# Sliding windows by DMA alone: twelve staged batches in place of eleven, and copies in fewer, larger DMAs

## The chip, the cores and the metric

The kernel runs on one core of a Trainium2 chip. The metric is the device time of one execution in microseconds (us), lower is better. A core has 16 DMA engines that move the data; SP (SyncE), ACT (ScalarE) and POOL (GpSimd) issue DMAs into queues of their own, called q1, q10 and q0 in the profile. [...]

## What is computed

The input `x` has 32 batches of 4096 rows of 256 float32 values. Windows of 64 rows are taken every 32 rows, 127 to a batch, and copied out one after the other:

```python
n_windows = (length - window_size) // stride + 1
result = np.zeros((batch, n_windows, window_size, dim), dtype=np.float32)
for i in range(n_windows):
    start = i * stride
    result[:, i] = x[:, start:start + window_size].copy()
```

Neighbouring windows share half of their rows. With blocks of 32 rows (32 KB), batch `b` has 128 blocks, and window `w` is block `w` (its half 0) followed by block `w + 1` (its half 1). The output has 127 x 2 blocks per batch, 266.3 MB in all. There is no arithmetic.

## The kernel before

There are two ways for a batch to get to the output. A *direct* batch is copied from HBM to HBM: each output block is one read and one write. A *staged* batch is loaded once into a tile of SBUF, `xb0` to `xb5`, with block `p` in partition `p`, and the tile is stored twice, once as the half 0 of all windows and once as the half 1.

A tile holds 128 blocks, but there are 127 windows. Each store thus writes one block too many, into the last window of the batch before or the first of the batch behind. The direct copies leave out some windows next to a staged batch, the *edges*, and write them once the stores that spill into them have landed.

Eleven batches are staged, 1, 4, ... 31 (L121), the other 21 are direct. Three queues work side by side:

- ACT (`ring_s`) runs `Staging.run` (L96 to L103): six loads, then the twelve stores of these tiles, then five loads, then ten stores. A load into a tile that was used before waits for its stores (`stored`, L83), a store for its load (`loaded`, L88). A load or a store is one DMA of 4 MB whose packets are 16 KB (`IN`, `OUT`, L9).
- SP (`ring_d`) copies 112 windows of each direct batch, 16 windows at a time (L144 to L162). Either one DMA moves both halves (`windows`, L29) or two DMAs move one half each. The counter `share` chooses: the second form is used often while ACT loads and seldom while it stores. Packets are 32 KB.
- POOL (`ring_r`) waits for the semaphore `near`, which counts a DMA just before the end of SP's list (L164), and then copies the edges in order of batches, 15 windows a DMA. Before each edge it waits for the stores that spill into it (`wait_stored`, L170).

At the end POOL copies most of the last direct batch's edge, part of it in 4 KB pieces (`columns`, L40, L179). SP waits for the stores of the last tile (L180), copies the last two windows, which such a store spilled into, as `columns` too (L181), and waits for all semaphores (L182, L183).

Of the kernel before, what the change touches and what calls it, by code (L numbers as in the profile page):

```python
# [6 lines left out]


DIRECT, IN, OUT = 32768, 16384, 16384  # L9


class Copier:


    def __init__(self, x, out, B, L, D, W, S, n_win):
        assert W == 2 * S and L % S == 0
        self.x, self.out = x, out
        self.B = B
        self.blk = S * D
        self.nb = L // S  # L20
        self.nw = n_win
# [7 lines left out]
    def windows(self, q, b, w0, n, half=None, piece=DIRECT):  # L29
# [7 lines left out]
            max_dma_last_dim=piece,  # L37
        )

    def columns(self, q, b, w0, n):  # L40

        part = self.blk // 8
        row = [1, part]
        return q.dma_start(  # L44
            out=self.oap((b * self.nw + w0) * 2, [[part, 16], [2 * self.blk, n], row]),
            in_=self.xap(b * self.nb + w0, [[part, 16], [self.blk, n], row]),
        )

    def load(self, q, t, b, shift):

        return q.dma_start(
            out=t[:, :],
            in_=self.xap(b * self.nb - shift, [[self.blk, self.nb], [1, self.blk]]),
            max_dma_last_dim=IN,
        )

    def store(self, q, t, b, half, shift):


        w = b * self.nw - half - shift  # L60
        return q.dma_start(
            out=self.oap(2 * w + half, [[2 * self.blk, self.nb], [1, self.blk]]),
            in_=t[:, :],
            max_dma_last_dim=OUT,
        )


class Staging:


    def __init__(self, c, tc, pool, dtype, batches, bufs, shifts):
        self.c, self.batches, self.shifts = c, batches, shifts
        self.tiles = [pool.tile([128, c.blk], dtype, name=f"xb{i}") for i in range(bufs)]
        self.loaded = [tc.alloc_semaphore(f"loaded{i}") for i in range(bufs)]
        self.stored = [tc.alloc_semaphore(f"stored{i}") for i in range(bufs)]

    def shift(self, g):
        return self.shifts.get(self.batches[g], 0)

    def load(self, q, g):  # L80
        n, i = divmod(g, len(self.tiles))
        if n:
            q.wait_ge(self.stored[i], 32 * n)  # L83
        self.c.load(q, self.tiles[i], self.batches[g], self.shift(g)).then_inc(self.loaded[i], 16)

    def store(self, q, g):
        n, i = divmod(g, len(self.tiles))
        q.wait_ge(self.loaded[i], 16 * (n + 1))  # L88
        for half in (0, 1):
            self.c.store(q, self.tiles[i], self.batches[g], half, self.shift(g)).then_inc(self.stored[i], 16)  # L90

    def wait_stored(self, q, g):
        n, i = divmod(g, len(self.tiles))
        q.wait_ge(self.stored[i], 32 * (n + 1))  # L94

    def run(self, q):  # L96
        bufs = len(self.tiles)
        for first in range(0, len(self.batches), bufs):
            group = range(first, min(first + bufs, len(self.batches)))
            for g in group:  # L100
                self.load(q, g)
            for g in group:
                self.store(q, g)  # L103


@with_exitstack
def kernel(
    ctx: ExitStack,
    tc: tile.TileContext,
    x: bass.AP,  # L110
    window_size: bass.AP,
    stride: bass.AP,
    out: bass.AP,
):
    nc = tc.nc
    W, S = int(window_size), int(stride)
    B, L, D = x.shape
    n_win = (L - W) // S + 1
    assert out.shape == (B, n_win, W, D)
    c = Copier(x, out, B, L, D, W, S, n_win)  # L120
    staged = [*range(1, B, 3)]  # L121
    direct = [b for b in range(B) if b not in staged]
    pool = ctx.enter_context(tc.tile_pool(name="xb", bufs=1))

    st = Staging(c, tc, pool, x.dtype, staged, 6, {0: -1, B - 1: 1})
    ring_d, ring_s, ring_r = nc.sync, nc.scalar, nc.gpsimd
    done = tc.alloc_semaphore("done")
    near = tc.alloc_semaphore("near")  # L130
    rest = tc.alloc_semaphore("rest")
    total = {done: 0, near: 0, rest: 0}

    def count(dma, sem):
        dma.then_inc(sem, 16)
        total[sem] += 16

    per, loads, stores = 6, 6 * 17, 34
    todo = 7 * len(direct)
    turns = share = 0  # L140
    with tc.tile_critical():  # L141
        st.run(ring_s)

        for b in direct:  # L144
            w = 0 if b - 1 not in staged else 8 if b + 1 in staged and b + 1 < B - 1 else 15
            for j in range(7):
                todo -= 1
                sem = near if todo == 2 else done
                share += 90 if turns % (loads + per * stores) < loads else 12
                if share >= 120:  # L150
                    share -= 120
                    turns += 4
                    count(c.windows(ring_d, b, w, 16, 0), done)
                    count(c.windows(ring_d, b, w, 16, 1), sem)
                else:
                    turns += 3
                    count(c.windows(ring_d, b, w, 16), sem)
                w += 16
                if todo == 7:
                    count(c.windows(ring_d, B - 1, c.nw - 1, 1, 1, 2048), done)  # L160
                    if 0 in staged:
                        count(c.windows(ring_d, 0, 0, 1, 0, 2048), done)  # L162

        ring_r.wait_ge(near, 16)  # L164
        pieces = (32768,)
        last = B - 2
        for i, b in enumerate(direct[:-1]):
            for g, n in enumerate(staged):
                if abs(n - b) == 1:
                    st.wait_stored(ring_r, g)  # L170
            parts = [(0, 15)] if b - 1 in staged else [(112, 15)]
            if b - 1 in staged and b + 1 in staged:
                parts = [(0, 8), (120, 7)]
            for w, n in parts:
                count(c.windows(ring_r, b, w, n, None, pieces[i % len(pieces)]), rest)


        count(c.windows(ring_r, last, 112, 4), rest)
        count(c.columns(ring_r, last, 116, 9), rest)  # L179
        st.wait_stored(ring_d, len(staged) - 1)  # L180
        count(c.columns(ring_d, last, 125, 2), done)  # L181
        for sem in (done, near, rest):  # L182
            ring_d.wait_ge(sem, total[sem])  # L183


# [33 lines left out]
```

## Time and profile before

| what | value |
|---|---|
| median of nine runs | 745.01 us (743.46 to 747.39) |
| the profiled execution | 745.01 us |
| its span, first to last instruction | 743.2 us |
| loads from ACT | 11 DMAs of 4096 KB, median 123.3 us from issue to landing |
| stores from ACT | 22 DMAs of 4096 KB, 141.7 us |
| copies from SP, both halves | 96 DMAs of 1024 KB, 100.3 us |
| copies from SP, one half | 102 DMAs of 512 KB, 90.0 us |
| edges from POOL | 20 DMAs of 960 KB, 37.7 us, and two smaller ones |
| wait of POOL for `near` | 646.4 us |

The profile lists every packet that a DMA engine moved, with its queue, size and duration, but not its engine. Its tables of slices and stretches add these packets up: "DMA share" is the sum of their durations over 16 engines' time, "GB/s" the bytes. Neighbouring packets of one engine overlap by a few nanoseconds, so a share can read 1.01. The packets under 512 B are semaphore writes, 16 for each DMA. The time from issue to landing is long because a DMA waits in its ring behind those issued before it.

### The profile page before, as it was taken

How to read it: one execution, taken by the hardware profiler on the slowest of the kernel's cores; microseconds unless marked ns; L12 is line 12 of the kernel's file. 1: busy time of each engine (PE TensorE's matmuls, PEld its weight loads, DVE VectorE, ACT ScalarE, POOL GpSimd, SP SyncE). 2: the span in 40 equal slices, each digit the busy share in tenths (PEclk: the TensorE clock that was granted, in tenths of full speed). 3: DMA queues.
4: the chain of work that ended last, by engine and by line, in shares of the span. 5: the costliest groups of instructions: out<-in, count | busy, mean ns of one | idle time of the engine just before them, and what ended most of it. 6: DMA issues, size and time to landing. Idle time of an engine off the chain costs nothing.

```text
span 743.2 us, 309 instructions
## 1 busy us (share of the span) xinstructions
POOL 12.8 (2%) x26
## 2 busy tenths in 40 slices
POOL 0000000000000000000000000000000000130100
DMA  8999999999999999999999999999999999999995
GB/s 369 433 429 423 430 433 429 431 421 434 424 423 425 430 419 426 430 421 432 424 429 416 409 428 433 436 428 435 430 431 427 424 433 429 426 429 433 424 431 240
DMA packets 18098, 313.26 MB, mean 421 GB/s; under 512 B 4144, under 2 KB 4144, under 8 KB 4336
## 3 DMA queue, kind: packets, MB, share of 16 engines
q1 hardware_dynamic: 7952, 154.32, 48.8%
q10 hardware_dynamic: 8976, 138.41, 44.0%
q0 software_dynamic: 1168, 20.51, 6.5%
q14 instruction: 2, 0.02, 0.0%
HBM read 220.95 MB, written 267.09 MB: 657 GB/s over the span
## 4 chain that ended last, share of the span: by engine, by line
another core or an unknown queue 92%; POOL 2%; issue 0%; POOLq 0%; SPq 0%
POOL out_dram L34 2%; POOL out_dram L44 0%; POOLq L214 0%; POOLq L94 0%; SPq L141 0%
## 5 line engine op out<-in xcount | busy, mean ns | idle before, releaser
L34 POOL DMA_DIRECT2D out_dram<-in_x_dram x21 | 12.0, 575 | 686.2 <-DMA out_dram<-in_x_dram 646.4
L44 POOL DMA_DIRECT2D out_dram<-in_x_dram x1 | 0.6, 581 | 0.0
L200 POOL MEMSET const-float32-0.0<- 128x1 f32 x1 | 0.1, 98 | 0.2 <-issue 0.2
L200 POOL MEMSET const-bfloat16-1.0<- 128x1 bf16 x1 | 0.1, 101 | 0.0
L200 POOL MEMSET const-uint8-127<- 128x1 uint8 x1 | 0.1, 99 | 0.0
L200 POOL MEMSET const-float32-1.0<- 128x1 f32 x1 | 0.1, 98 | 0.0
## 6 DMA issues: line engine op xcount, KB each, us to landing
out_dram<-in_x_dram SPq DMA_DIRECT2D x96, 1024.0 KB, 100.3
out_dram<-xb ACTq DMA_DIRECT2D x22, 4096.0 KB, 141.7
out_dram<-in_x_dram SPq DMA_DIRECT2D x102, 512.0 KB, 90.0
xb<-in_x_dram ACTq DMA_DIRECT2D x11, 4096.0 KB, 123.3
out_dram<-in_x_dram POOLq DMA_DIRECT2D x20, 960.0 KB, 37.7
out_dram<-in_x_dram POOLq DMA_DIRECT2D x1, 576.0 KB, 40.4
out_dram<-in_x_dram POOLq DMA_DIRECT2D x1, 256.0 KB, 36.9
out_dram<-in_x_dram SPq DMA_DIRECT2D x1, 128.0 KB, 2.4
```

The lines of the kernel that those rows point to most:

```text
L34: return q.dma_start(out=self.oap((b * self.nw + w0) * 2 + h, [[2 * blk, n], row]), in_=self.xap(b * self.nb + w0 + h, [[blk, n], row]), m ...
L44: return q.dma_start(out=self.oap((b * self.nw + w0) * 2, [[part, 16], [2 * self.blk, n], row]), in_=self.xap(b * self.nb + w0, [[part, 16 ...
L200: nc = _bacc.Bacc("TRN2", target_bir_lowering=False, num_devices=1)
```

## The change

- Twelve batches are staged, 0, 3, 6, 9, 11, ... 31, and twenty direct. Batch 0 is loaded one block further on and batch 31 one block further back, so that nothing spills over the ends of the tensors; one block of each is copied alone (`singles`).
- Loads and stores have packets of 32 KB. A load is two DMAs, one for the even and one for the odd partitions (`split(2)`); a store is two of each half in the same way. The stores of the last three tiles are eight DMAs per half, each of 16 partitions, every eighth one (`split(8)`).
- The stores of the last tile are ordered anew: half 1 first, then an eighth of half 0, all counted by `stored`; the other seven eighths are counted by a new semaphore, `ended`. SP's last two windows wait for `stored` alone.
- SP's copies are made by `many`: one DMA moves one half of 112 windows, 7 packets on each of 16 engines. The counter `share` is gone, and so are the DMAs with both halves. The last of these DMAs is cut in two, and `near` counts the second-last.
- The edge of the last direct batch is 3 whole windows and 10 in `columns`, in place of 4 and 9; the others are as before for the new set of batches.
- `quarters` is defined but not called.

```diff
-DIRECT, IN, OUT = 32768, 16384, 16384
+DIRECT, IN, OUT, REST = 32768, 32768, 32768, 32768
...
+    def many(self, q, b, w0, n, half):
+        return q.dma_start(
+            out=self.oap((b * self.nw + w0) * 2 + half, [[2 * self.blk, 16], [32 * self.blk, n], [1, self.blk]]),
+            in_=self.xap(b * self.nb + w0 + half, [[self.blk, 16], [16 * self.blk, n], [1, self.blk]]),
+        )
...
+    def load(self, q, t, b, c, rows):
+        p, step, n, unit = rows
+        return q.dma_start(
+            out=t[p : p + (n - 1) * step + 1 : step, :],
+            in_=self.xap(b * self.nb + c + p // unit, [[step // unit * self.blk, n], [1, self.blk]]),
             max_dma_last_dim=IN,
         )
...
+    def store(self, q, t, b, c, rows, half):
+        p, step, n, unit = rows
+        w = b * self.nw + c + p // unit - half
+        return q.dma_start(
+            out=self.oap(2 * w + half, [[2 * step // unit * self.blk, n], [1, self.blk]]),
+            in_=t[p : p + (n - 1) * step + 1 : step, :],
             max_dma_last_dim=OUT,
         )
...
     def load(self, q, g):
...
+        i = g % len(self.tiles)
+        if self.count[self.stored[i]]:
+            q.wait_ge(self.stored[i], self.count[self.stored[i]])
+        for rows in self.split(2):
+            self.issue(self.c.load(q, self.tiles[i], *self.items[g], rows), self.loaded[i])
+        self.after_load[g] = self.count[self.loaded[i]]
+
+    def split(self, parts):
+        return [(k, parts, 128 // parts, 1) for k in range(parts)]
 
     def store(self, q, g):
...
+        q.wait_ge(self.loaded[i], self.after_load[g])
+        split = self.split(8 if g >= len(self.items) - 3 else 2)
+        parts, end = [(rows, half) for half in (0, 1) for rows in split], []
+        if g == len(self.items) - 1:
+            parts = [(rows, 1) for rows in split] + [(split[0], 0)]
+            end = split[1:]
+        for rows, half in parts:
+            self.issue(self.c.store(q, self.tiles[i], *self.items[g], rows, half), self.stored[i])
+        for rows in end:
+            self.issue(self.c.store(q, self.tiles[i], *self.items[g], rows, 0), self.ended)
...
-    staged = [*range(1, B, 3)]
+    staged = [0, 3, 6, 9, 11, 14, 17, 20, 22, 25, 28, 31]
+    items = [(b, 1 if b == 0 else -1 if b == B - 1 else 0) for b in staged]
...
-    per, loads, stores = 6, 6 * 17, 34
-    todo = 7 * len(direct)
-    turns = share = 0
...
+        main += [(b, w + 16 * j, min(7, 7 - j), half) for j in range(0, 7, 7) for half in (0, 1)]
+        if b == last:
+            edges.append((b, 112, 3))
+        elif before and behind:
+            edges += [(b, 0, 8), (b, 120, 7)]
+        else:
+            edges.append((b, 0 if before else 112, 15))
...
+    b, w, n, half = main.pop()
+    main += [(b, w, n - 1, half), (b, w + 16 * (n - 1), 1, half)]
     with tc.tile_critical():
         st.run(ring_s)
...
+        for i, (b, w, n, half) in enumerate(main):
+            count(c.many(ring_d, b, w, n, half), near if i == len(main) - 2 else done)
...
+        for b, w, n in edges:
+            for k in (b - 1, b + 1):
+                if k in place and b != last:
+                    st.wait_stored(ring_r, place[k])
+            count(c.windows(ring_r, b, w, n, None, REST), rest)
...
+        count(c.columns(ring_r, last, 115, 10), rest)
+        st.wait_stored(ring_d, place[B - 1])
         count(c.columns(ring_d, last, 125, 2), done)
-        for sem in (done, near, rest):
-            ring_d.wait_ge(sem, total[sem])
+        total[st.ended] = st.count[st.ended]
+        for sem, n in total.items():
+            ring_d.wait_ge(sem, n)
```

More of the change, by code (lines that the diff above doesn't have):

```diff
@@ L38, in windows, with quarters @@
         )
+    def quarters(self, q, b, w0, p0, n):
+        part = self.blk // 4
+        at = p0 * 2 * part
+        dims = [[n * part, 2], [1, n * part]]
+        return q.dma_start(
+            out=bass.AP(self.out.tensor, self.oap((b * self.nw + w0) * 2, dims).offset + at, [[2 * self.blk, 4], *dims]),
+            in_=bass.AP(self.x.tensor, self.xap(b * self.nb + w0, dims).offset + at, [[self.blk, 4], *dims]),
+            max_dma_last_dim=4 * n * part,
+        )
[3 more added lines that the diff above has]
+            in_=self.xap(b * self.nb + w0 + half, [[self.blk, 16], [16 * self.blk, n], [1, self.blk]]),
+        )
     def columns(self, q, b, w0, n):
@@ L47, in columns @@
         )
-    def load(self, q, t, b, shift):
+    def load(self, q, t, b, c, rows):
+        p, step, n, unit = rows
         return q.dma_start(
-            out=t[:, :],
-            in_=self.xap(b * self.nb - shift, [[self.blk, self.nb], [1, self.blk]]),
+            out=t[p : p + (n - 1) * step + 1 : step, :],
+            in_=self.xap(b * self.nb + c + p // unit, [[step // unit * self.blk, n], [1, self.blk]]),
             max_dma_last_dim=IN,
         )
-    def store(self, q, t, b, half, shift):
-        w = b * self.nw - half - shift
+    def store(self, q, t, b, c, rows, half):
+        p, step, n, unit = rows
+        w = b * self.nw + c + p // unit - half
         return q.dma_start(
-            out=self.oap(2 * w + half, [[2 * self.blk, self.nb], [1, self.blk]]),
-            in_=t[:, :],
+            out=self.oap(2 * w + half, [[2 * step // unit * self.blk, n], [1, self.blk]]),
+            in_=t[p : p + (n - 1) * step + 1 : step, :],
             max_dma_last_dim=OUT,
@@ L68, with __init__ @@
 class Staging:
-    def __init__(self, c, tc, pool, dtype, batches, bufs, shifts):
-        self.c, self.batches, self.shifts = c, batches, shifts
+    def __init__(self, c, tc, pool, dtype, items, bufs):
+        self.c, self.items = c, items
         self.tiles = [pool.tile([128, c.blk], dtype, name=f"xb{i}") for i in range(bufs)]
@@ L75, in __init__ @@
         self.stored = [tc.alloc_semaphore(f"stored{i}") for i in range(bufs)]
-    def shift(self, g):
-        return self.shifts.get(self.batches[g], 0)
-    def load(self, q, g):
[L81 to L84, printed above, removed]
-    def store(self, q, g):
[L87 to L90, printed above, removed]
+        self.ended = tc.alloc_semaphore("ended")
@@ new lines, in __init__, with issue @@
+        self.count = {sem: 0 for sem in (*self.loaded, *self.stored, self.ended)}
+        self.after_load, self.after_store = {}, {}
+    def issue(self, dma, sem):
+        dma.then_inc(sem, 16)
+        self.count[sem] += 16
+    def load(self, q, g):
+        i = g % len(self.tiles)
[4 more added lines that the diff above has]
+        self.after_load[g] = self.count[self.loaded[i]]
@@ new lines, in split @@
+    def split(self, parts):
+        return [(k, parts, 128 // parts, 1) for k in range(parts)]
+    def store(self, q, g):
+        i = g % len(self.tiles)
+        q.wait_ge(self.loaded[i], self.after_load[g])
[8 more added lines that the diff above has]
+            self.issue(self.c.store(q, self.tiles[i], *self.items[g], rows, 0), self.ended)
+        self.after_store[g] = self.count[self.stored[i]]
@@ L92, in wait_stored @@
     def wait_stored(self, q, g):
-        n, i = divmod(g, len(self.tiles))
-        q.wait_ge(self.stored[i], 32 * (n + 1))
+        q.wait_ge(self.stored[g % len(self.tiles)], self.after_store[g])
     def run(self, q):
         bufs = len(self.tiles)
-        for first in range(0, len(self.batches), bufs):
-            group = range(first, min(first + bufs, len(self.batches)))
+        for first in range(0, len(self.items), bufs):
+            group = range(first, min(first + bufs, len(self.items)))
@@ L120 @@
     c = Copier(x, out, B, L, D, W, S, n_win)
-    staged = [*range(1, B, 3)]
+    staged = [0, 3, 6, 9, 11, 14, 17, 20, 22, 25, 28, 31]
+    items = [(b, 1 if b == 0 else -1 if b == B - 1 else 0) for b in staged]
+    place = {b: g for g, b in enumerate(staged)}
     direct = [b for b in range(B) if b not in staged]
     pool = ctx.enter_context(tc.tile_pool(name="xb", bufs=1))
-    st = Staging(c, tc, pool, x.dtype, staged, 6, {0: -1, B - 1: 1})
+    st = Staging(c, tc, pool, x.dtype, items, 6)
     ring_d, ring_s, ring_r = nc.sync, nc.scalar, nc.gpsimd
@@ L136, in count @@
         total[sem] += 16
-    per, loads, stores = 6, 6 * 17, 34
-    todo = 7 * len(direct)
-    turns = share = 0
+    main, edges, singles = [], [], [(B - 1, c.nw - 1, 1)]
+    if 0 in staged:
+        singles.append((0, 0, 0))
+    last = B - 2
+    for b in direct:
+        before, behind = b - 1 in staged, b + 1 in staged
+        w = 15 if before and (not behind or b == last) else 8 if before else 0
+        if b == last:
+            w = 0
+        main += [(b, w + 16 * j, min(7, 7 - j), half) for j in range(0, 7, 7) for half in (0, 1)]
+        if b == last:
+            edges.append((b, 112, 3))
[3 more added lines that the diff above has]
+            edges.append((b, 0 if before else 112, 15))
@@ L141 @@
+    b, w, n, half = main.pop()
+    main += [(b, w, n - 1, half), (b, w + 16 * (n - 1), 1, half)]
     with tc.tile_critical():
         st.run(ring_s)
[L144 to L162, printed above, removed]
@@ L164 @@
-        ring_r.wait_ge(near, 16)
[L165 to L175, printed above, removed]
@@ L178 @@
-        count(c.windows(ring_r, last, 112, 4), rest)
-        count(c.columns(ring_r, last, 116, 9), rest)
-        st.wait_stored(ring_d, len(staged) - 1)
+        for i, (b, w, n, half) in enumerate(main):
+            count(c.many(ring_d, b, w, n, half), near if i == len(main) - 2 else done)
+            if i == len(main) // 2:
+                for b, w, half in singles:
+                    count(c.windows(ring_d, b, w, 1, half, 2048), done)
+        ring_r.wait_ge(near, 16)
+        for b, w, n in edges:
[3 more added lines that the diff above has]
+            count(c.windows(ring_r, b, w, n, None, REST), rest)
```

## The prediction

> **What bounds the kernel now.** The kernel only moves data, so I read the DMA rows of the page first, then the queues, then stretches of the span, and last the end.
>
> ```profile
> POOL 12.8 (2%) x26
> ...
> DMA  8999999999999999999999999999999999999995
> GB/s 369 433 429 423 430 433 429 431 421 434 424 423 425 430 419 426 430 421 432 424 429 416 409 428 433 436 428 435 430 431 427 424 433 429 426 429 433 424 431 240
> DMA packets 18098, 313.26 MB, mean 421 GB/s; under 512 B 4144, under 2 KB 4144, under 8 KB 4336
> ```
>
> No engine computes. All 16 DMA engines are busy in every slice but the last, at 409 to 436 GB/s. Time is therefore (packets x time of a packet) / 16, plus the ends.
>
> ```profile
> q1 hardware_dynamic: 7952, 154.32, 48.8%
> q10 hardware_dynamic: 8976, 138.41, 44.0%
> q0 software_dynamic: 1168, 20.51, 6.5%
> ...
> HBM read 220.95 MB, written 267.09 MB: 657 GB/s over the span
> ```
>
> q1 is SP's queue (direct copies), q10 ACT's (loads and stores of staged batches), q0 POOL's (edges). The shares add up to 99.3%: the engines are the bound. A staged batch costs 384 blocks of 32 KB on the engines (128 loaded, 256 stored) and 384 of HBM traffic; a direct one costs 254 blocks on the engines but 508 of HBM traffic. So staging helps only if HBM holds the engines up. The stretches of the span tell whether it does (us, POOL busy, clock, DMA share, GB/s):
>
> ```profile
> 126.00:402.00 276.00, 0.00 (x0) 1.00 1.01 427
> 402.00:420.00 18.00, 0.00 (x0) 1.00 1.01 398
> 420.00:510.00 90.00, 0.00 (x0) 1.00 1.01 431
> 510.00:655.00 145.00, 8.12 (x15) 1.00 1.00 429
> 655.00:733.00 78.00, 4.43 (x8) 1.00 1.00 428
> 733.00:740.00 7.00, 0.00 (x0) 1.00 0.36 145
> 740.00:743.20 3.20, 0.00 (x0) 1.00 0.01 3
> ```
>
> In the second group's loads (420 to 510) the engines reach 431. While q10 stores they run at 427 to 429, and where stores give way to loads (402 to 420) at 398. The share stays at 1.01: the packets themselves get longer. After 733 the engines stand idle for 64% of 7 us, 4.5 us. The end, from the timeline and SP's waits:
>
> ```profile
> 737.87 0.58 SPq L44 DMA_DIRECT2D out_dram<-in_x_dram  x1
> ```
> ```profile
> SPq L44 <- DMA out_dram<-xb: 179.2, 1, 179.2
> ```
>
> SP's last two windows (L181) are issued only when the last store has landed, into empty engines.
>
> The packet records give prices. Median packet: 1213 ns for 32 KB, 611 ns for 16 KB. What packets take above these medians is 8.0 us per engine in all: 0.7 before 12 us, 0.8 in the rest of the first loads, 3.4 in 126 to 402, 1.5 in 402 to 420, 0.1 in 420 to 510, 0.9 to 655, 0.5 to 733. I call this the excess. In 56 stretches of 5 us without it, a least-squares fit of the packet counts to engine time gives what a packet really occupies (neighbours overlap slightly): 1209.8 ns for 32 KB, 606.8 for 16 KB, 6.0 for a semaphore write.
>
> Sum for before, per engine: 5312 x 1209.8 / 16 = 401.7, 8448 x 606.8 / 16 = 320.4, 4 KB and 2 KB packets 1.9, 4144 semaphore writes 1.6: 725.5. Start 2.0 (first packet), excess 8.0, end 3.3 (last packet at 739.9 to the end of the span), which leaves 4.4 for the tail; the 4.5 us of idle above confirm it. Total 743.2, the span; the execution took 745.01, 1.8 more, and that is also the median of the nine runs.
>
> [...] an engine takes turns between queues packet by packet. The trace agrees if a semaphore write takes a turn as well: between 126 and 402 us the records show q1 at 245 GB/s and q10 at 181, a ratio of 1.35, and two 32 KB packets plus a semaphore against three 16 KB packets give 1.33. [...]
>
> **The change, part by part.**
>
> Twelve staged batches: 12 x 384 + 20 x 254 + 2 = 9690 blocks against 11 x 384 + 21 x 254 + 1 = 9559. 131 more x 1209.8 / 16 = +9.9 us on full engines. Nothing hides it.
>
> 32 KB packets for loads and stores: two of 16 KB cost 1213.6, one of 32 KB 1209.8; 4224 x 3.8 / 16 = -1.0 us.
>
> Fewer semaphores: `many` needs 41 DMAs on SP where there were 198; with 108 on ACT (24 loads, 36 + 48 stores) and 23 on POOL it makes 175, 2800 writes against 4144: -0.5 us.
>
> Base after: 9664 blocks x 1209.8 / 16 = 730.7, 4 KB and 2 KB packets 2.1, semaphores 1.1: 733.9, that is +8.4. With start 2.0 and end 3.3, 739.2 plus excess plus tail. Before paid 8.0 + 4.4 = 12.4 for these two, so the change must bring them to 4.0 to break even.
>
> Start: engines are full of q10's loads from 3 us on, so direct copies that begin before 5.8 us only displace loads: 0.
>
> Tail: the last tile signals `stored` nine sixteenths through, so SP's last columns go out with 7 stores an engine, 8.5 us, still queued: they vanish under them. What stays is how unequally the engines finish. Before, they ran dry from 733.5, on the mean at 734.9, all but one or two by 736.5, the last at 738.6. I take 2.0 (ends 1.3 and 3.7).
>
> Excess: turns in the new kernel are 7 data + 1 semaphore on q1, 4 + 1 on q10, so q1 : q10 = 0.875 : 0.8, about 226 : 206 GB/s (229 : 202 is what the two had from 420 to 510). HBM traffic in the store phase, twice q1 plus q10, falls from 672 to 658 GB/s. In 5 us pieces of 126 to 402 the excess was 0.02 to 0.18% where q1 had under 54% of the bytes, 0.9 to 2.6% above; a correlation of 0.55, no more, and in the first loads there was none. I take half the store rate: 243 us of stores at 0.45% = 1.1, the second stores 0.5, start 0.7, first loads 0.7, the switch to loads 0.8 (half, since it comes in two DMAs), second loads 0.1, edges with stores 0.6: 4.5 us. Ends: 1.5 if equal packets and shares calm it, 9 if 32 KB bursts hit HBM harder.
>
> POOL's waits cost 0: `near` falls at about 645 us by the count of turns (321 of q1's against 396 of q10's), and q10 then has about 37 packets an engine to fill every gap; edges that wait for tiles 9 and 10 come late in POOL's list. The store waits on ACT stand behind five queued tiles, as now.
>
> Sum: 739.2 + 4.5 + 2.0 = 745.7 span, 747.5 in all.
>
> **The rivals.** A (0.50): the above, 745.5 to 751; extra blocks are not fully repaid. For it: 431 is already reached today, so little is left to gain. Against it: my halving rests on a weak correlation.
>
> B (0.33), not slower: the balance of the queues is the mechanism. With q1 and q10 at nearly equal shares and equal packets, the store phase behaves as 420 to 510 does: excess 1.5, tail 1.3, 742.0 span, 743.8 in all (742.3 to 745.5). It decides once excess and tail together fall below 4.0. For it: 0.1 us of excess in 90 us at just this balance. Against: those were loads, and the first loads at the same balance had 0.8 in 114.
>
> C (0.17), much slower: [...] In the last three tiles each DMA touches every eighth partition[...]; q10 works there about 40% of an engine's time, so 48 packets x 0.4 x 0.6 us (half a packet's wait) = 11.5 us more: 757.2 span, 759 in all[...]. Against: SP's and POOL's packets fill the gaps.
>
> That the change fails to do what it says: earlier direct copies do nothing, as worked out; it is in every case.
>
> **How the numbers follow.** Likeliest A: 747.5. The range is 742.7 to 755.5; below lies the best of B (0.05), above most of C's worst (0.1). A measurement here tells 0.2%, 1.5 us, from no change. Faster than 743.5: half of B, 0.17. Within: the other half of B and A's low edge, 0.25. Slower: 0.58.
>
> **What would show it.** Bytes 317.5 MB and about 2800 packets under 512 B; stretches with loads and with stores at 431 to 433 GB/s under B, 428 to 431 under A; the last twenty microseconds without a hole before SP's columns; under C, 16-row stores at visibly lower GB/s from about 610 us on. I am wrong if the store phase shows no excess at all, or if 32 KB packets from SBUF take longer than 1213 ns at the median.

## The result, and the profile after

The changed kernel takes 759.72 us (758.79 to 763.79, nine runs) against 744.81 us for the kernel before. The ratio is 1.0204, with a 95% interval of 1.0192 to 1.0216: slower by 2.0%. The span of the profiled execution is 757.8 us against 743.2, 14.6 more.

First the slices of the page of the changed kernel, and its queues:

```profile
DMA  8999999999999999999999999999999999999995
GB/s 367 436 429 425 436 431 425 434 431 431 434 432 434 425 439 431 429 439 427 420 431 434 422 434 431 436 432 426 439 429 431 436 413 400 377 367 415 427 401 223
DMA packets 12817, 317.54 MB, mean 419 GB/s; under 512 B 2928, under 2 KB 2928, under 8 KB 3152
...
q10 hardware_dynamic: 6336, 151.00, 47.3%
q1 hardware_dynamic: 5248, 147.00, 45.3%
q0 software_dynamic: 1232, 19.53, 6.3%
...
HBM read 216.86 MB, written 267.19 MB: 639 GB/s over the span
```

The engines are as full as before, and the bytes are the forecast 317.5 MB. The first 32 slices average 429 GB/s, where before it was 425; from the 33rd on they fall, to 367 at the lowest. A slice is 18.9 us, so the fall begins near 610 us. Stretches of the changed kernel (us, POOL busy, clock, DMA share, GB/s):

```profile
120.00:360.00 240.00, 0.00 (x0) 1.00 1.00 432
490.00:610.00 120.00, 0.00 (x0) 1.00 1.00 432
610.00:655.00 45.00, 0.00 (x0) 1.00 1.00 409
659.00:665.00 6.00, 6.00 (x12) 1.00 1.05 273
665.00:742.00 77.00, 5.76 (x11) 1.00 1.00 409
742.00:755.00 13.00, 0.00 (x0) 1.00 0.52 219
```

The two store phases (first two lines) run at 432 GB/s, where the old ones had 427 and 429. At about 610 us the stores of the last three tiles begin, the ones in eighths. Between 659 and 665 us SP's list is done and POOL's edges have hardly begun: q10 is almost alone, and the engines, fully busy, move 273 GB/s, 229 of them for q10. The same place in pieces of 2 us:

```profile
655.00:657.00 2.00, 0.00 (x0) 1.00 1.08 344
657.00:659.00 2.00, 1.15 (x2) 1.00 0.97 328
659.00:661.00 2.00, 2.00 (x5) 1.00 1.16 311
661.00:663.00 2.00, 2.00 (x5) 1.00 1.03 262
663.00:665.00 2.00, 2.00 (x4) 1.00 0.97 246
```

From the timeline of the changed kernel:

```profile
657.85 10.70 POOL L34 DMA_DIRECT2D out_dram<-in_x_dram  x19 [657.41 <-DMA out_dram<-in_x_dram]
...
729.85 0.59 SPq L62 DMA_DIRECT2D out_dram<-in_x_dram  x1
```

POOL's wait for `near` ends at 657.4, but the first packet of its queue starts only at 662.6. SP has only one packet an engine left behind `near` here; before, its copies reached into the first edges. SP's last columns now go out at 729.85, well before the end, as the change has it. Still the engines run dry only one by one, from 742 to 754.3 us (52% busy in the last line of stretches).

The packet records complete the account. Excess, which is again what packets take above 1213 ns for 32 KB, is 13.0 us per engine: 3.6 before 610 us, 2.4 from 610 to 655, 3.5 to 665, and 3.5 to 742. The tail, the time that is lost while the engines run dry one after the other, is what the other terms leave: 5.1 us. So against before: packets +8.4 (as worked out beforehand), excess 13.0 - 8.0 = +5.0, tail 5.1 - 4.4 = +0.7, start +0.3 (first packet at 2.3 us), end +0.2. That is the 14.6 us. As the tail is a remainder, the sum alone doesn't prove it; the engines' idle time after 742 us (4.9 us, and 4.2 after 733 us before) gives the same +0.7.

### The profile page after: what moved, and what is told of

The parts are those of the page before. It is cut to its first block, busy times and chain, and to the rows that moved or that the text cites. A ratio compares the mean times of both kernels' runs of the same rounds, so it can differ in the third digit from the quotient of the medians.

```text
span 757.8 us, 234 instructions
## 1 busy us (share of the span) xinstructions
POOL 13.1 (2%) x27
## 2 busy tenths in 40 slices
DMA packets 12817, 317.54 MB, mean 419 GB/s; under 512 B 2928, under 2 KB 2928, under 8 KB 3152
## 4 chain that ended last, share of the span: by engine, by line
another core or an unknown queue 92%; POOL 1%; issue 0%; POOLq 0%; SPq 0%
POOL out_dram L34 1%; POOL out_dram L62 0%; POOLq L252 0%; SPq L199 0%; POOLq L132 0%
## 5 line engine op out<-in xcount | busy, mean ns | idle before, releaser
L34 POOL DMA_DIRECT2D out_dram<-in_x_dram x22 | 12.4, 568 | 697.8 <-DMA out_dram<-in_x_dram 657.4
```

What stands on the lines that cost most here:

```text
L34: return q.dma_start(out=self.oap((b * self.nw + w0) * 2 + h, [[2 * blk, n], row]), in_=self.xap(b * self.nb + w0 + h, [[blk, n], row]), m ...
```

## The experiments

**Stores by themselves.** One tile, loaded once and stored twice in each of seven forms, with nothing beside it. The forms, as lists of (first partition, step, count, partitions per block):

```diff
...
+    forms = [
+        [(0, 1, 128, 1)],
+        st.split(2),
+        st.split(4),
+        st.split(8),
+        [(16 * k, 1, 16, 1) for k in range(8)],
+        [st.split(8)[k] for k in (0, 4, 1, 5, 2, 6, 3, 7)],
+    ]
...
```

The sixth is `split(8)` in another order, the seventh `split(8)` into neighbouring rows of the output.

> This kernel computes no windows beyond a few: it loads one tile of 128 blocks and stores it twice in each of seven forms, one form after the other, with nothing beside it; the rest of the output is not written. 8.4 MB a form. Theory [...]: one DMA of 128 partitions, two of 64 and four of 32 run at 400 to 430 GB/s, 20 us each; eight of every eighth partition at about 217 GB/s, 39 us; eight of 16 neighbouring partitions[...] at about 109 GB/s, 77 us; every eighth partition [...] between 217 and 430; every eighth partition into dense rows of the output again at 217, since the output's addresses do not matter. Rival (the output's rows 512 KB apart, or one semaphore per packet): neighbouring partitions are no slower than every eighth, and dense rows bring every eighth partition back to 400 or more.

The 217 and 109 GB/s of the theory are a half and a quarter of the 433 or so that full engines move; that eighths would fall to the half and neighbouring partitions to the quarter was the author's estimate. One stretch within each form, in this order, from a single execution:

```profile
16.00:32.00 16.00, 0.00 (x0) 1.00 0.99 426
37.00:54.00 17.00, 0.00 (x0) 1.00 0.98 420
59.00:76.00 17.00, 0.00 (x0) 1.00 1.01 432
80.00:112.00 32.00, 0.00 (x0) 1.00 1.00 227
120.00:160.00 40.00, 0.00 (x0) 1.00 0.92 190
167.00:190.00 23.00, 0.00 (x0) 1.00 0.99 319
195.00:228.00 33.00, 0.00 (x0) 1.00 0.97 220
```

Whole tiles, halves and quarters run at 420 to 432 GB/s, eighths at 227. Dense rows of the output do not help (220), so the output's addresses are not the cause. The number of DMAs and of semaphore writes isn't either: the same eighths in another order reach 319. It matters which partitions a DMA takes (432 for quarters, 227 for eighths) and which DMA follows which (319). One number of the theory fell: 16 neighbouring partitions gave 190, not 109. Why the partitions matter is not shown by these runs.

**The last three tiles in halves.**

```diff
-        split = self.split(8 if g >= len(self.items) - 3 else 2)
+        split = self.split(2)
```

> The changed kernel with the last three tiles stored in two DMAs per half like all others. Theory [...]: what the packets take above 1213 ns after 610 us falls from 9.5 to about 1 us per engine, and the engines end closer together, tail 5.4 to 2.5 us: span about 746, 748 in all. Rival (twelve batches with 32 KB packets overload HBM once the edges run): stays above 755.

756.83 us: the theory missed by 9 us, and the number is the rival's (above 755). Stretches of this kernel, and below them a short one in which q10 is alone:

```profile
610.00:660.00 50.00, 0.00 (x0) 1.00 1.00 433
665.00:715.00 50.00, 9.62 (x18) 1.00 1.00 415
717.00:745.00 28.00, 0.00 (x0) 1.00 0.99 334
```

```profile
661.00:665.00 4.00, 3.28 (x6) 1.00 1.03 442
```

The loss at 610 us is gone (433). Between SP's list and the edges, 661 to 665 us, q10 is alone here too, and now it moves 442 GB/s. But from 717 us on the engines move 334 GB/s. By then q10 has run out: with one semaphore write behind four packets, in place of one behind each, its stores take their turns faster: in the changed kernel the bytes of q1 to those of q10 are 1.10 while q10 stores in halves (490 to 610 us) and 1.52 while it stores in eighths (610 to 655). What remains are edges, copies from HBM to HBM, and these alone reach only the 334. One loss had hidden another. A smaller one, 1.9 us of excess from 660 to 715 us while edges run beside stores, isn't explained by either.

**The last three tiles in quarters** (`split(4 if ... else 2)`), and **in eighths of another order**, and **of neighbouring partitions**:

> The changed kernel with the last three tiles stored in four DMAs per half, 32 partitions each. They keep the full rate alone (430 GB/s when tried by themselves) and put one semaphore write behind two packets, so q10 stays behind longer than with halves. Theory (two losses at the end: [...] direct copies left alone with halves, which run at about 330 GB/s): [...] the edges are alone for less time than the 30 us seen with halves: 748 to 753. Rival (twelve batches are slow at the end however they are stored): 755 to 760.

> The changed kernel with the eighths of the last three tiles in the order 0, 4, 1, 5, 2, 6, 3, 7[...]. Theory [...] the loss after 610 us is at least halved, 748 to 754 in all. Rival (size of the DMAs or number of semaphore writes): no difference, 759 to 761.

> The changed kernel with the last three tiles stored in eight DMAs per half of 16 neighbouring partitions. Theory [...] q10 at no more than 109 GB/s, the last 25 MB need some 230 us from 610 us on: 830 or more. Rival (size of the DMAs, semaphores, HBM): no difference, 757 to 762.

Quarters: 759.48 us, a miss, and within the rival's range; 428 GB/s from 610 to 660 us, but 338 from 722 to 742, with the edges alone again. So stores that run at full rate by themselves did not make this kernel faster. The other order: 755.50 us, between the theory's 748 to 754 and the rival's 759 to 761, and its four runs spread from 751.77 to 761.26, so it decides little. Neighbouring partitions: 762.80 us in a single execution, not 830: just above the rival's range. Such stores reached about 190 GB/s by themselves, and q10 has 190 beside the edges as well (665 to 735 us).

**Direct copies by themselves.** Is it HBM that holds the lone edges up, or POOL's queue with its DMAs of 15 rows?

```diff
+        for b in (0, 1):
+            for half in (0, 1):
+                count(c.many(ring_d, b, 0, 7, half), done)
...
+        for k in range(16):
+            count(c.windows(ring_r, 4 + k // 8, 15 * (k % 8), 15), rest)
```

> This kernel makes a few windows only, in four stretches one after the other: four half-batch copies from SP with nothing beside them; two batches from SP with both halves in one DMA; sixteen edges of 15 windows from POOL alone; four half-batch copies from SP beside four tile halves stored from ACT. The rest of the output is not written. Theory (direct copies alone hold up at HBM, whoever issues them): all of the first three at 320 to 350 GB/s, the last at 430. Rival (POOL's queue, with 15 rows on 16 engines, is what is slow alone): the first two at 430, only POOL's at about 330.

Its four stretches: `many` from SP, both halves from SP, edges from POOL, `many` beside stores.

```profile
18.00:52.00 34.00, 0.00 (x0) 1.00 0.97 328
62.00:98.00 36.00, 0.00 (x0) 1.00 1.01 340
112.00:148.00 36.00, 3.35 (x6) 1.00 0.99 329
168.00:222.00 54.00, 0.00 (x0) 1.00 0.99 428
```

Direct copies alone reach 328 to 340 GB/s whether SP or POOL issues them, and half and half with stores 428, in a single execution. It is the kind of copy, not the queue; what holds such copies up is not shown.

**The edges earlier.** Halves throughout, and `near` counted six DMAs before the end of SP's list:

```diff
-            count(c.many(ring_d, b, w, n, half), near if i == len(main) - 2 else done)
+            count(c.many(ring_d, b, w, n, half), near if i == len(main) - 6 else done)
```

> The changed kernel with halves for all tiles, and the semaphore that starts the edges six DMAs from the end of SP's list in place of two, so that the edges run beside the staged queue and never alone. Theory (the extra blocks cost 8.4 us[...]): excess about 5 us and tail about 2: span 746, 748 in all, still slower than before by some 3 us. Rival (the edges themselves are slow, alone or not): no better than 755.

755.26 us: the expectation was missed by 7 us, and the number is the rival's. From 610 to 680 us the three queues together move 407 GB/s. By the count of turns two of three are direct copies then, so the loss was brought forward, not avoided.

**Partitions apart from balance.** The last three tiles in halves, but with 16 KB packets. By the count of turns q10 then moves about as slowly as with eighths, while each DMA takes every second partition:

```diff
-        split = self.split(8 if g >= len(self.items) - 3 else 2)
+        split = self.split(2)
+        piece = 16384 if g >= len(self.items) - 3 else OUT
...
```

> The changed kernel with the last three tiles stored in two DMAs per half, but in packets of 16 KB, for these tiles alone. By turns q10 then moves 64 KB in 9 turns of an engine, about as slowly as with eighths (32 KB in 2), and outlasts the edges[...]. Theory [...]: 610 to 655 us at 420 or more in place of 409, no dip under 300 when q10 is alone, no lone edges; excess 5 to 7 us, 748 to 752 in all. Rival (the end is slow because of its balance[...]): 756 to 760.

751.41 us, 8.3 less than the changed kernel. (A half is 128 KB an engine in 9 turns, not 64: eight packets and a semaphore write. That is 14 KB a turn, against 16 with eighths.) Stretches:

```profile
610.00:655.00 45.00, 0.00 (x0) 1.00 1.00 407
659.00:665.00 6.00, 5.91 (x11) 1.00 1.03 442
665.00:720.00 55.00, 3.34 (x6) 1.00 1.01 430
```

From 655 us on the loss is gone: 442 and 430 GB/s against 273 and 409, an excess of 0.5 us against 7.0. Of the 7.0 us, 3.5 fall before 665 us, nearly all on q10's own packets. Halves of 32 KB packets lost nothing in that place (442 GB/s), so these 3.5 us are the price of the eighths. The 3.5 us after 665 are less clear: 2.1 of them lie on packets of the edges, and halves and quarters of 32 KB packets, beside edges, had an excess of 1.9 and 1.4 us in some 50 us as well. The smaller packets may have removed a part of it; no run separates the two.

And 610 to 655 us stays at 407, where the expectation said 420 or more. So this part of the loss (2.6 us of excess here, 2.4 in the changed kernel) does not come from the eighths: q1 has 61% of the bytes there, and 60% with eighths.

**Eleven or twelve batches.** The old kernel with the new list of twelve batches and nothing else:

```diff
-    staged = [*range(1, B, 3)]
+    staged = [0, 3, 6, 9, 11, 14, 17, 20, 22, 25, 28, 31]
```

> The kernel before with the change's list of twelve staged batches and nothing else of it. Theory (a staged batch more costs 9.9 us of packets, and only the shares of the queues decide what comes back): 131 blocks more, excess 7 to 9 us as before, 752 to 757. Rival (the twelfth batch pays for itself): 742 to 747.

757.29 us, 12.2 more than the 745.05 of the kernel before beside it, and just past the range: 9.9 us of packets, 1.5 of excess (9.5 against 8.0) and a somewhat longer tail. The twelfth batch does not pay for itself. Nearly all of the 14.9 us by which the change is slower is this batch: all else in it adds 2.4 us (759.72 against 757.29), its gains in packets and in the store phase against its loss at the end.

The change with eleven batches (the new code, the old list) was run in five forms: loads and stores in quarters; stores in quarters, with the edges early or late; halves with 16 KB packets for the last five or four tiles.

> Eleven staged batches, as in the kernel before, with all else of the change, loads and stores in four DMAs of 32 partitions each. Theory (bytes are the main cost): base 724.0 + 2.0 + 3.3 and 7 us of excess, since q1 has 57% of the bytes as before, tail 2: span 738, 740 in all, 0.7% faster than before. Rival (the twelfth batch pays for itself by sparing HBM): not under 745.

> Eleven staged batches, loads in two DMAs and stores in four, the edges started six DMAs before the end of SP's list. Same base as the other version with eleven. Theory: excess 6 to 8 us, with direct copies at 70% of the bytes for the last 60 us; 739 to 742 in all. Rival: as for the other.

> Eleven staged batches, loads in two DMAs and stores in four, edges started at the end of SP's list as in the change. By turns q10 has some 25 packets an engine left when q1 is done and the edges 37, so some 13 us of edge copies are left alone at 330 GB/s and cost 4 us more. Theory: base 729.3 with start and end, excess 7 + 5, tail 2: 743 span, 745 in all, equal to before. Rival (early or late edges make no difference): 747.5 as with the early ones.

> Eleven staged batches, halves for all tiles, 16 KB packets for the stores of the second group of five tiles. By turns q10 has 410 and q1 337, so that q10 outlasts the edges. Base 729.6 with start and end. Theory (bytes, and direct copies beside staged ones until the end): excess about 8, tail 2.5: span 740, 741.5 to 743.5 in all, faster than before. Rival (q1 at 66% of the bytes in the second stores overloads HBM): 747 or more.

> The same with 16 KB packets for the stores of the last four tiles, 394 turns for q10. Same theory: 741 to 744; the edges may be alone for some 5 us. Rival: 747 or more.

They took 752.94, 747.67, 750.96, 751.80 and 754.36 us. All are slower than before: every forecast of a gain was wrong, and the rivals' numbers (not under 745, 747 or more) held. Late edges cost 3.3 us more than early ones, near the forecast 4. Their excess is 14 to 19 us, where the kernel before, with just as much to copy directly, has 8.0. Most of these forms leave some stretch with too large a share of direct copies: late edges are alone at 338 GB/s for 26 us, early ones make 397 beside q1, and 16 KB packets leave q1 66% of the bytes and 402 for 110 us.

**The last store alone.** The kernel before, with the last tile's stores in the new order and `ended`:

```diff
...
+        self.c.store(q, self.tiles[i], self.batches[g], 1, self.shift(g)).then_inc(self.stored[i], 16)
+        for odd in (0, 1):
+            sem = self.ended if odd else self.stored[i]
+            self.c.store(q, self.tiles[i], self.batches[g], 0, self.shift(g), odd).then_inc(sem, 16)
```

> The kernel before with the last tile's stores in the change's order alone: half 1 first, then the even and the odd partitions of half 0, the odd ones counted by a semaphore of their own, so that SP's last columns are issued with 2 MB of stores still queued. Theory: the hole of 738.6 to 739.9 us and part of the wait go, 1 to 2.5 us faster than before, 742.5 to 744. Rival (the tail is the spread of the engines only): no difference, within 0.1%.

744.41 us against 745.05, a ratio of 0.9992 (0.9983 to 1.0001): not to be told from no change, as the rival had it. SP's columns go out at 729.98 us instead of 737.87, but the last packet lands at 738.4 instead of 739.9. No version tried is faster than the kernel before beyond doubt.

## Why the prediction was wrong

The forecast was 747.5 us (742.7 to 755.5); the measured time lies above the range. Its direction was right, and so was most of the sum.

- **Packets: right.** 131 blocks more, larger packets and fewer semaphores were put at +8.4 us. The bytes came out as counted. There were 2928 packets under 512 B, not about 2800: POOL's queue has 128 more than 16 for each of its 23 DMAs (64 more before), which is less than 0.1 us per engine. Of the readings, one is loose: the first slice, at 369 GB/s, is below 409 as well as the last.
- **Earlier direct copies: nothing came of them, as said. POOL's waits: right in part.** `near` fell at 657 us rather than 645, of which 6 us are the excess until then. The later wait of 40.4 us for a tile's stores left no hole: q10 and queued edges filled it. The wait for `near` did cost something, as the step that failed shows.
- **Excess up to the last tiles: right.** The terms before "edges with stores" add up to 3.9 us; measured to 610 us were 3.6. The store phase is calmer with nearly equal shares: an excess of 0.28% from 120 to 362 us, where 126 to 402 had 1.24%. The bursts of 32 KB did no harm there: the median packet from SBUF stays at 1213 ns.
- **"Edges with stores 0.6": the step that failed.** It took the last 25 MB of stores as more of the same. Measured are 9.5 us after 610, in three parts. The first, 2.4 us until 655, stays when the eighths go: q10, with one semaphore write behind each packet, falls back, and q1 has 60% of the bytes. The prediction had counted q10's turns (396) and used them for POOL's waits, but had not carried the new ratio, 0.875 : 0.5 by the count (1.75; measured 1.52), into the excess. The second, 3.5 us from 655 to 665, breaks "POOL's waits cost 0" too: q10 was to "fill every gap" with its last packets, and it did keep the engines busy between SP's list and the edges, but eighths by themselves move about half of what whole tiles do (227 GB/s against 426). The third, 3.5 us after 665, goes with the eighths as well; how much of it is due to the partitions and how much to the size of the packets stays open.
- **Tail "2.0": too small.** It is 5.1 us, and 4.6 in the run with 16 KB packets. The wait for SP's columns was taken for a large part of the old tail; the run with the last store alone (744.41 us against 745.05) shows that the tail is mainly the engines' unequal ends.

Rival C named the stores of every eighth partition, the place and nearly the time, 759 us, and the sign that it gave, slower stores from about 610 us on, appeared, clearly so from 655 on. The nearness of the time is in part luck. C put 11.5 us on these stores alone, with a wait of half a packet that was the author's estimate, beside a tail of 2.0 and nothing for the shares of the queues; measured are 3.5 to 7.0 us of excess (8.3 us of time in all with 16 KB packets), and the rest of the miss is the first part above and the longer tail. C's own time lay outside the range that the prediction gave.

The argument used against C, that SP's and POOL's packets fill the gaps, held while SP's packets were there: up to 655 us the loss is the same with 16 KB halves. It failed when they were not. Between 655 and 664 us q10 was nearly alone, and its median packet took 1.93 us in place of 1.21. The trace of the kernel before, which moves whole tiles only, could not weigh C; the stores by themselves, at 227 GB/s, could have.

Rival B's balance was real, with 432 GB/s in the store phases, but only up to the last three tiles. It brought the excess until 610 us to 3.6, from 7.1 before, and those 3.5 us are less than 8.4 us of packets.

## What to carry to other kernels

When DMA engines are full, add the packets first: the twelfth staged batch spares traffic in HBM, but cost 9.9 us of packets and won none of it back (757.29 us against 745.05). Follow the balance of the queues to the last packet, by turns and with semaphore writes among them, because taking one loss away may only uncover the next, as the halves did (433 GB/s from 610 us on, then 334 from 717). And measure a new shape of transfer by itself before it goes into the part of the kernel where nothing is left to hide it.

## What the runs showed of the hardware

- Copies from HBM to HBM alone: 328 to 340 GB/s from SP's queue and from POOL's, with engines that reach 432 when half of the bytes are stores from SBUF.
- In between, in long stretches of direct copies beside stores, the rate falls with the share of direct copies among the bytes: 432 GB/s at 51%, 427 at 57%, 407 at 61%, 402 at 66%, about 330 at 100%. 432 is about what full engines move (433, from 1209.8 ns for 32 KB). Counted as HBM traffic, which is the rate times one plus the share, the other four are 670, 655, 667 and 660 GB/s: nearly one number, though no run measures by itself what HBM can move. The 670 are the kernel before. Short stretches where one pattern gives way to another can be slower (398 GB/s from 402 to 420 us before).
- Stores from SBUF by themselves, as several DMAs one behind the other: every eighth partition 227 GB/s, 16 neighbours 190, every second or fourth partition 420 to 432. The same eighths in another order: 319.
- A semaphore write occupies an engine for only 6.0 ns by the fit, but the shares of the queues come out right if it takes a turn between queues: counted 1.33 and measured 1.35 for q1 to q10 before (126 to 402 us), counted 1.97 and measured 1.98 with eleven batches and 16 KB packets for five tiles (490 to 600 us), counted 1.09 and measured 1.10 in the changed kernel with halves (490 to 610 us). With eighths (610 to 655 us) the count gives 1.75, and 1.52 was measured. So the number of DMAs moves the shares of the queues.
